# Sums of w_down's blocks formed during the first up projection and staged operand by operand: a hybrid decoder layer on one core

## The chip, the cores and the metric

The kernel runs on one core of one Trainium2 chip, as one program of some 31,800 instructions. The metric is device time in microseconds (us) of one execution, from the start of the program to its end; lower is better. Five engines work side by side, each in its own order: TensorE (PE in the rows, its weight loads PEld), VectorE (DVE), ScalarE (ACT), GpSimd (POOL) and SyncE (SP), which here issues all the transfers of the layer's second part. Their instructions meet through semaphores only.

## What is computed

One layer of a hybrid decoder for 2048 prompt tokens and 32 sample tokens: a combined projection feeds an S5 mixer and a gated linear attention, both go through w_o, and a ConvFFN follows. The change touches the ConvFFN alone (D = 1024, d_ff = 2816 = 22 blocks of 128):

```python
h2 = rms_norm(x, ffn_norm)
a, b = jnp.split(h2 @ w_up, 2, axis=-1)
ext = jnp.concatenate([conv0.astype(a.dtype), a], axis=1)
a_conv = conv_b
for w in range(CONV_W):
    a_conv = a_conv + conv_w[w] * ext[:, w:w + T]
x = x + (jax.nn.silu(a_conv) * b) @ w_down
```

Everything is float32. Each product is made of three passes of TensorE over operands that were split into a rounded part (hi) and a rest (lo): hi*hi, hi*lo, lo*hi.

## The kernel before, in words

**The stages.** The mixers and w_o take the first 1250 us or so. Then comes the up projection of the first half of the tokens (`up_first`, called for fb = 0 to 21, one block of 128 channels of a and of b each; three pieces of 352 columns, 48 matmuls each). Its results, the gated activations, go to DRAM as gT. The second half of the tokens goes through the up projection as 22 items ("up", j), and the down projection follows as 4 x 8 items ("down", c, j): c is a chunk of w_down's rows, j a block of 256 tokens. The chunks hold 2 * KH[c] blocks of 128 rows, KH = (2, 3, 3, 3), from row block K0[c] on.

**Seven products.** An item is a 2 x 2 block product by a scheme of Strassen's kind with seven products, made in the order 1, 2, 3, 6, 4, 7, 5; products 3 and 4 in this order belong to the item before (`last`). A product of chunk 0 is 6 matmuls of 512 columns, one of chunks 1 to 3 is 9, one of an up item 12. Each product p takes a stationary operand, prepared for each item one item ahead by `Item.step` and `prepare`, and a moving operand `R[p]`, which stays the same for all items of a chunk. After a product the next one is emitted, and only then `follow(p)`, which reads the PSUM bank: for products 1, 6 and 5 ScalarE copies it into a half tile (`S.get("H")`, t_H or pair_L in the rows; the bank is all) and VectorE adds that to the residual (r1, r2: t_L tiles loaded from x2d by `res_load(j + 1)` after product 7); the other products are added from the bank directly. The finished rows go back to x2d.

**The moving operands.** For a chunk of w_down with the four blocks b11, b12, b21, b22 (upper and lower rows, left and right 512 columns), products 1, 2, 3 use b11, b21, b22 as they are, product 7 uses b12 - b22 (`difference`), and 6, 4, 5 use sums built on it in place (`sums`). `operand(p, to)` forms the sum on VectorE, copies the block to hi on ScalarE and subtracts to lo on VectorE (`split2`), in two parts, 1024 elements a partition for the first two row blocks and 512 for the third. The raw blocks lie in six tiles `raw` (four for chunk 0), loaded all together by `down_blocks`. For chunks 1 to 3 a background generator, `gen_raw_down`, loads them from item j = 2 on and forms the differences. In the last item of a chunk (`end`) each operand is replaced right after the product that used it for the last time: this is called the exchange here. At the end of the up items the raw blocks are loaded after product 2, the differences formed after product 7, and all operands wait in the list `late` for product 7 or 5.

**What sets the order.** One program order is written by the Python loop; `Background.tick` puts steps of the generators between the products by priority and by an estimate of each engine's time. SP issues its transfers strictly in that order; one whose tile is not free yet holds up all that are behind it. Tiles come from `Slots`: 43 whole tiles L of 1024 floats a partition and 6 half tiles H. `get("H")` takes a small tile or a half of a split L tile (pair_L); `open()` counts what is free. All engine operations go through one helper, so all rows have its line, L290. "M" asks for a whole tile.

## Time and profile before

| | before |
|---|---|
| median of 3 timed runs | 2475.72 us (2470.17 to 2477.51) |
| the profiled execution | 2471.15 us |
| its span in the trace | 2469.4 us |
| busy: TensorE matmuls / weight loads | 93% / 79% |
| busy: VectorE / ScalarE / GpSimd | 62% / 36% / 22% |
| mean granted clock of TensorE | 0.96 of full speed |
| DMA, mean | 133 GB/s |

The span is cut into stretches in the table of windows below: its columns are the stretch and its length in us, busy us (and instructions) of PE, PEld, DVE, ACT and POOL, the granted TensorE clock (1.00 is 2.4 GHz), the mean busy share of the 16 DMA engines, and GB/s. In a timeline a row is a run of instructions of one kind without a gap: start, us, engine, line, operation, out<-in, shape and count, and in brackets the idle time ahead of it with what ended it. An all is a PSUM bank, t_L and pair_L are tiles of the pool L, t_H one of H. The first-half up projection lies at about 1260 to 1470, the up items at 1480 to 1940, the down projection from there to the end, its chunks beginning at about 1940, 2060, 2190 and 2330.

### The profile page before, as it was taken

To read this page: it belongs to the slowest core of one execution; us is meant where nothing else is said; L and a number is where in the kernel's file an instruction comes from. 1 tells how busy PE (TensorE), PEld (TensorE's weight loads), DVE (VectorE), ACT (ScalarE), POOL (GpSimd) and SP (SyncE) were. 2 spreads that over 40 slices of the span, in tenths; PEclk is the share of its full clock that TensorE was granted. 3 is DMA by queue.
4 is the path that set the end of the run, shared out by engine and by line. 5 is a ranking of instruction groups with operands and counts; after the bars stand their busy time and mean duration, and the time that the engine had idled before them with its cause. 6 is when DMAs were issued, how large, how long until landed. Compare 5 with 4: busy or idle time off the path is not lost.

```text
span 2469.4 us, 31818 instructions
## 1 busy us (share of the span) xinstructions
PE 2305.9 (93%) x11809; PEld 1950.0 (79%) x11809; DVE 1538.3 (62%) x2727; ACT 898.6 (36%) x1634; POOL 538.5 (22%) x645
## 2 busy tenths in 40 slices
PE   7898999899999799999989998999999787989898
PEld 5677777677877699999989996887888565767677
DVE  7777457765533476654454336666666777676777
ACT  3242244444422633342151114444434333242444
POOL 5254325545422345521011100000000000000011
PEclk9899999989999899999989999999999898989999
DMA  6134455427453815435422212232223474646544
GB/s 167 60 101 136 135 158 160 124 87 222 133 166 121 270 49 150 113 112 167 145 99 78 68 55 68 78 93 86 77 77 102 146 255 148 231 158 222 179 159 155
DMA packets 345260, 327.99 MB, mean 133 GB/s; under 512 B 55410, under 2 KB 273706, under 8 KB 345104
## 3 DMA queue, kind: packets, MB, share of 16 engines
q1 hardware_dynamic: 344752, 325.81, 42.6%
q8 instruction: 93, 1.52, 0.3%
q14 instruction: 63, 0.52, 0.1%
q10 hardware_dynamic: 352, 0.15, 0.0%
HBM read 230.81 MB, written 95.08 MB: 132 GB/s over the span
## 4 chain that ended last, share of the span: by engine, by line
PE 59%; DVE 18%; ACT 7%; issue 4%; POOL 2%; DMA 1%; SPq 0%; POOLq 0%; ACTq 0%; DVEq 0%
PE all L290 40%; DVE t_L L290 14%; PE mm L290 12%; PE bg L290 8%; ACT t_L L290 6%; DVE t_H L290 2%; DVE pair_L L290 2%; POOL t_H L290 2%; POOL t_L L290 1%; DMA t_L<-x2d 0%; SPq L290 0%; ACT t_H L290 0%; DMA ydT<-t_L 0%; POOL pair_L L290 0%; DMA t_H<-in_x_prompt_dram 0%
## 5 line engine op out<-in xcount | busy, mean ns | idle before, releaser
L290 PE MATMUL all<-t_L,t_L 128*128 128x512 f32 (+4 forms) x7358 | 1495.2, 365 | 80.8 <-ACT t_L L290 24.8
L290 PEld LDWEIGHTS all<-t_L,t_L 128*128 128x128 f32 (+2 forms) x7358 | 1296.7, 191 | 272.3 <-DVE t_L L290 37.5
L290 DVE TENSOR_TENSOR t_L<-t_L,t_L 128x1024 fp32r<-128x1024 f32 (+7 forms) x649 | 567.0, 902 | 178.1 <-ACT t_L L290 157.0
L290 ACT ACTIVATE t_L<-t_L 128x1024 fp32r<-128x1024 f32 (+9 forms) x471 | 374.4, 817 | 480.8 <-DVE t_L L290 399.8
L290 PE MATMUL mm<-t_L,t_L 128*128 128x512 f32 (+2 forms) x2160 | 493.2, 385 | 14.3 <-DVE t_L L290 12.3
L290 PEld LDWEIGHTS mm<-t_L,t_L 128*128 128x128 f32 (+1 forms) x2160 | 383.7, 191 | 100.0 <-issue 17.7
L290 POOL TENSOR_SCALAR rr<-ss 128x1 f32<-128x1 f32 (+1 forms) x51 | 19.7, 387 | 1098.9 <-ACT t_H L290 1093.6
L290 DVE TENSOR_TENSOR t_L<-t_L,all 128x512 f32<-128x512 f32 (+2 forms) x268 | 172.3, 643 | 112.9 <-PE all L290 51.8
L290 POOL TENSOR_SCALAR t_L<-t_L 128x1024 fp32r<-128x1024 f32 (+1 forms) x91 | 116.6, 1287 | 319.8 <-PE all L290 113.8
L290 POOL TENSOR_TENSOR t_L<-t_L,t_L 128x1024 fp32r<-128x1024 f32 x49 | 136.4, 2786 | 51.0 <-ACT t_L L290 38.8
L290 ACT ACTIVATE t_L<-all 128x512 f32<-128x512 f32 (+2 forms) x134 | 71.6, 539 | 185.9 <-PE all L290 185.5
L290 DVE TENSOR_TENSOR t_L<-t_L,t_H 128x512 f32<-128x512 f32 (+4 forms) x148 | 90.2, 611 | 77.0 <-ACT t_H L290 49.8
L290 DVE SCALAR_TENSOR_TENSOR t_L<-all,cw,t_L 128x351 f32<-128x351 f32 (+1 forms) x132 | 74.9, 567 | 72.5 <-ACT t_L L290 71.7
L290 ACT ACTIVATE t_H<-all 128x512 f32<-128x512 f32 (+2 forms) x105 | 61.5, 589 | 155.7 <-PE all L290 155.4
L290 PE MATMUL bg<-t_L,t_L 128*128 128x256 f32 (+7 forms) x628 | 110.0, 341 | 2.3 <-DVE t_H L290 2.3
L290 PEld LDWEIGHTS bg<-t_L,t_L 128*128 128x128 f32 (+4 forms) x628 | 84.1, 181 | 24.4 <-issue 10.9
L290 ACT ACTIVATE t_L<-all,cw 128x352 f32<-128x352 f32 x66 | 42.4, 642 | 165.8 <-PE all L290 161.0
L290 ACT ACTIVATE t_L<-bg 128x512 fp32r<-128x512 f32 (+7 forms) x121 | 53.5, 462 | 106.3 <-PE bg L290 103.9
L290 DVE SCALAR_TENSOR_TENSOR t_L<-t_L,cw,t_L 128x1024 f32<-128x1024 f32 x44 | 56.5, 1285 | 24.6 <-ACT t_L L290 23.8
L290 ACT ACTIVATE t_H<-t_L 128x1024 bf16<-128x1024 f32 (+2 forms) x60 | 57.0, 959 | 28.1 <-DVE t_L L290 18.2
L290 ACT ACTIVATE junk<-bg 128x128 bf16<-128x128 f32 (+1 forms) x68 | 18.8, 276 | 117.1 <-PE bg L290 115.5
L290 ACT ACT_TABLE_LOAD x41 | 52.6, 1283 | 23.1 <-DVE t_L L290 14.8
(178 smaller groups left out, 1608.9 us busy)
## 6 DMA issues: line engine op xcount, KB each, us to landing
t_L<-in_w_up_dram SPq DMA_DIRECT2D x88, 512.0 KB, 4.8
t_L<-x2d SPq DMA_DIRECT2D x80, 512.0 KB, 5.7
t_L<-in_w_in_dram SPq DMA_DIRECT2D x64, 512.0 KB, 5.7
x2d<-t_L SPq DMA_DIRECT2D x48, 512.0 KB, 3.2
gT<-t_L SPq DMA_DIRECT2D x44, 512.0 KB, 2.7
t_L<-gT SPq DMA_DIRECT2D x48, 384.0 KB, 4.1
t_L<-in_w_o_dram SPq DMA_DIRECT2D x24, 512.0 KB, 5.3
t_L<-in_w_down_dram SPq DMA_DIRECT2D x22, 512.0 KB, 4.4
```

Source lines behind the costliest of these rows:

```text
L290: r = fn(*args, **kw)
```

## The change

Two things are done. First, a background generator `gen_sums` runs beside `up_first`. For each of the 11 pairs of row blocks (upper and lower half of a chunk) it loads two whole rows of blocks of w_down, forms the four blocks 12 - 22, 11 + (12 - 22), and so on with four VectorE operations of 512, and stores the two tiles to a new DRAM tensor `Wd`. Second, `raw`, `Columns`, `down_blocks` and `gen_raw_down` are gone; `operand` now serves only the up items. `down_block` loads the block of a single operand, in the order of `STAGES`, from w_down for operands 1, 2 and 3 and from `Wd` for 6, 7, 5 and 4 (one whole tile, and a half tile for the third row block). `gen_stage_down` loads three of them from item j = 2 on; `down_operand` splits a staged block into hi and lo, gives its tiles back, and `next_block` then issues the load of the next. At the end of the up items the first two loads are issued after products 1 and 2, and operands are made from product 3 on. The list in `t = [S.get("M")] + [S.get("H")] * (kh - 2)` calls `S.get("H")` once also for kh = 2, where the result is not kept.

```diff
+    Wd = drp.tile([NF // 2, 2, P, SM], F32, tag="Wd", name="Wd")
...
-    def down_blocks(q):
-
-        kh = KH[q]
-        raw.extend(S.get("L") for _ in range(6 if kh == 3 else 4))
...
-    def gen_raw_down(q):
-        while raw or S.open() < 6.0 or S.whole() < 6:
-            yield "idle"
-        down_blocks(q)
-        yield raw
-        difference(Columns(q))
+    stage, staged = {}, []
+    STAGES = (1, 2, 6, 7, 5, 3, 4)
+
+    def down_block(p, q):
+
+        kh, k0 = KH[q], sum(KH[:q])
+        n = min(kh, 2)
+        t = [S.get("M")] + [S.get("H")] * (kh - 2)
+        if p in (1, 2, 3):
+            r0, c0 = (K0[q] + (kh if p > 1 else 0)) * P, 512 * (p == 3)
+            src = w_down[r0 : r0 + kh * P, c0 : c0 + 512].rearrange("(k p) c -> p k c", p=P)
+        else:
+            src = Wd[k0 : k0 + kh, p < 6, :, 512 * (p in (5, 7)) :][:, :, :512].rearrange("k p c -> p k c")
+        SP.dma_start(t[0][:, :1024].rearrange("p (k c) -> p k c", k=2), src[:, :2])
         if kh == 3:
...
+            SP.dma_start(t[1][:, :512], src[:, 2])
+        stage[p] = t
+        staged.append(p)
+
+    def next_block(q):
+        if len(staged) < 7:
+            down_block(STAGES[len(staged)], q)
+
+    def down_operand(p, q):
+
+        room_for(p, KH[q])
+        t = stage.pop(p)
+        split2(R[p][0][:, :1024], R[p][1][:, :1024], t[0][:, :1024])
+        if KH[q] == 3:
+            split2(R[p][2][:, :512], R[p][2][:, 512:1024], t[1][:, :512])
+        S.put(*t)
+
+    def gen_stage_down(q):
+
+        for p in STAGES[:3]:
+            while S.open() < 1.5 or S.whole() < 2:
+                yield "idle"
+            down_block(p, q)
+
+    def gen_sums():
+
+        for q in range(4):
+            for k in range(KH[q]):
+                while S.open() < 3.0 or S.whole() < 2 or not all(("st", 1, i) in flags for i in "abc"):
+                    yield "idle"
+                S_ = Share(S, 2.0)
+                a, b = S_.get("M"), S_.get("M")
+                for t, r in ((a, K0[q] + k), (b, K0[q] + KH[q] + k)):
+                    SP.dma_start(t[:, :D], w_down[r * P : (r + 1) * P])
+                yield a, b
+                lo, hi = slice(0, 512), slice(512, 1024)
+                sub(a[:, hi], b[:, hi], a[:, hi])
+                add(a[:, lo], a[:, lo], a[:, hi])
+                sub(b[:, hi], b[:, hi], a[:, lo])
+                sub(b[:, lo], b[:, lo], a[:, lo])
+                yield a, b
+                for i, t in enumerate((a, b)):
+                    SP.dma_start(Wd[sum(KH[:q]) + k, i], t[:, :SM])
...
             if p in (3, 4):
-                if refill:
-                    operand(p, refill)
-            elif end and kind == "up":
-                room_for(p, to)
+                if refill is not None:
+                    down_operand(p, refill)
+                    next_block(refill)
...
+            elif end:
+                room_for(p, KH[to])
+                if kind == "up":
+                    for q in {1: 2, 2: 2}.get(p, 0) * "x":
+                        next_block(to)
                 late.append(p)
...
-            elif end:
-                operand(p, to)
+                while late and late[0] in stage and (p not in (1, 2) or kind == "down"):
+                    q = late.pop(0)
+                    down_operand(q, to)
+                    next_block(to)
...
-                nxt = [bg.add(2, gen_raw_down(c + 1))]
+                nxt = [bg.add(2, gen_stage_down(c + 1))]
```

TensorE's order stays the same, instruction by instruction. VectorE in the last item of chunk 1, around product 6, before: t_L_17140 to t_L_17145 are the raw blocks, rows of 768 and 384 are the preparation of the next item, rows with all or t_H read a bank's result into the residual.

```order
L290 TENSOR_TENSOR t_L_17432<-t_L_17432,t_L_17574 128x384 x2
L290 TENSOR_TENSOR t_L_17452<-t_L_17452,all_17468 128x512
L290 TENSOR_TENSOR t_L_17639<-t_L_17432,t_L_17638 128x768
L290 TENSOR_TENSOR t_L_17140<-t_L_17141,t_L_17140 128x1024
L290 TENSOR_TENSOR t_L_13012<-t_L_17140,t_L_13011 128x1024
L290 TENSOR_TENSOR t_L_17144<-t_L_17144 128x512
L290 TENSOR_TENSOR t_L_16680<-t_L_17144,t_L_16680 128x512
L290 TENSOR_TENSOR t_L_17563<-t_L_17563,t_H_17657 128x512
```

The same place after: t_L_17238, 17242 and 17262 are staged blocks of operands 1, 2 and 6, pair_L_17239 and pair_L_15945 their half tiles.

```order
L290 TENSOR_TENSOR t_L_11359<-t_L_17238,t_L_11358 128x1024
L290 TENSOR_TENSOR t_L_16740<-pair_L_17239,t_L_16740 128x512
L290 TENSOR_TENSOR t_L_17654<-t_L_17654,pair_L_17701 128x512
L290 TENSOR_TENSOR t_L_17705<-t_L_17667,t_L_17704 128x768
L290 TENSOR_TENSOR t_L_11403<-t_L_17242,t_L_11402 128x1024
L290 TENSOR_TENSOR t_L_16762<-pair_L_17239,t_L_16762 128x512
L290 TENSOR_TENSOR t_L_17654<-t_L_17654,all_17691 128x512
L290 TENSOR_TENSOR t_L_17525<-t_L_17525,t_L_17667 128x384 x2
L290 TENSOR_TENSOR t_L_17545<-t_L_17545,all_17561 128x512
L290 TENSOR_TENSOR t_L_17738<-t_L_17525,t_L_17737 128x768
L290 TENSOR_TENSOR t_L_13123<-t_L_17262,t_L_13122 128x1024
L290 TENSOR_TENSOR t_L_16791<-pair_L_15945,t_L_16791 128x512
L290 TENSOR_TENSOR t_L_17656<-t_L_17656,pair_L_17758 128x512
```

The two sums (t_L_17140<-t_L_17141,t_L_17140 and t_L_17144<-t_L_17144) are gone from between the subtractions; the subtractions stand where they stood.

SyncE in the same exchange, before: the loads of the residuals from x2d and of the activations from gT, and the stores of finished rows.

```order
L290 DMA t_L_17561<-x2d 128x1024
L290 DMA t_L_17563<-x2d 128x1024
L290 DMA t_L_17663<-gT 128x6x128
L290 DMA t_L_17665<-gT 128x6x128
L290 DMA x2d<-t_L_17452 128x1024
L290 DMA x2d<-t_L_17454 128x1024
L290 DMA t_L_17706<-x2d 128x1024
L290 DMA t_L_17708<-x2d 128x1024
L290 DMA t_L_17786<-gT 128x6x128
L290 DMA t_L_17788<-gT 128x6x128
```

The same stretch of SyncE after; the rows with Wd or in_w_down_dram load staged blocks.

```order
L290 DMA t_L_17688<-Wd 128x2x512
L290 DMA pair_L_17239<-Wd 128x512
L290 DMA t_L_17712<-Wd 128x2x512
L290 DMA pair_L_17239<-Wd 128x512
L290 DMA x2d<-t_L_17545 128x1024
L290 DMA t_L_17745<-in_w_down_dram 128x2x512
L290 DMA pair_L_15945<-in_w_down_dram 128x512
L290 DMA t_L_17764<-gT 128x6x128
L290 DMA t_L_17766<-gT 128x6x128
L290 DMA x2d<-t_L_17547 128x1024
L290 DMA t_L_17787<-Wd 128x2x512
L290 DMA pair_L_17239<-Wd 128x512
```

Four blocks, each of a whole tile and a half tile, are now loaded between these; three of the four half tiles are the same one, pair_L_17239, so that each load of it stands behind the subtraction that reads it.

SyncE in the first-half up projection around fb = 13, before: t_L<-in_w_up_dram are the weights of a coming fb, gT<-t_L the results of one.

```order
L290 DMA t_L_11143<-in_w_up_dram 128x8x128
L290 DMA t_L_11149<-in_w_up_dram 128x8x128
L290 DMA gT<-t_L_10833 128x1024
L290 DMA gT<-t_L_10833 128x32
L290 DMA t_L_11472<-in_w_up_dram 128x8x128
L290 DMA t_L_11478<-in_w_up_dram 128x8x128
L290 DMA gT<-t_L_11151 128x1024
L290 DMA gT<-t_L_11151 128x32
```

The same stretch of SyncE after, with the pairs of w_down's rows and of Wd's tiles in it.

```order
L290 DMA t_L_11657<-in_w_up_dram 128x8x128
L290 DMA t_L_11701<-in_w_up_dram 128x8x128
L290 DMA gT<-t_L_11497 128x1024
L290 DMA gT<-t_L_11497 128x32
L290 DMA Wd<-t_L_11653 128x1024
L290 DMA Wd<-t_L_11654 128x1024
L290 DMA t_L_11798<-in_w_down_dram 128x1024
L290 DMA t_L_11799<-in_w_down_dram 128x1024
L290 DMA t_L_11864<-in_w_up_dram 128x8x128
L290 DMA Wd<-t_L_11798 128x1024
L290 DMA Wd<-t_L_11799 128x1024
L290 DMA t_L_11910<-in_w_down_dram 128x1024
```

Loads of w_down and stores of Wd have come between; each store of Wd waits for VectorE's four operations on its tile, and what is behind it on SP waits too.

## Rows read from the trace of the kernel before

**Rows 1.** The page's first part: busy us, share of the span, instructions.
```profile
PE 2305.9 (93%) x11809; PEld 1950.0 (79%) x11809; DVE 1538.3 (62%) x2727; ACT 898.6 (36%) x1634; POOL 538.5 (22%) x645
```
**Rows 2.** Windows: stretch, us, busy PE PEld DVE ACT POOL, PEclk, DMA share, GB/s.
```profile
1260.00:1300.00 40.00, 31.06 (x173) 29.95 (x172) 26.95 (x57) 20.80 (x43) 3.67 (x6) 0.83 0.05 18
1300.00:1440.00 140.00, 140.00 (x880) 140.00 (x879) 55.19 (x144) 21.57 (x43) 13.53 (x13) 1.00 0.23 72
1860.00:1920.00 60.00, 59.50 (x260) 48.34 (x259) 39.04 (x51) 25.68 (x33) 0.00 (x0) 1.00 0.33 107
1920.00:1960.00 40.00, 26.70 (x88) 19.43 (x87) 30.66 (x44) 14.39 (x21) 0.00 (x0) 0.83 0.36 110
1980.00:2040.00 60.00, 50.71 (x211) 40.45 (x209) 44.41 (x77) 22.30 (x42) 0.00 (x0) 0.91 0.79 260
2040.00:2080.00 40.00, 28.11 (x93) 21.08 (x94) 31.91 (x48) 16.36 (x25) 0.00 (x0) 0.79 0.36 118
2100.00:2160.00 60.00, 60.00 (x266) 47.57 (x265) 40.74 (x62) 17.53 (x27) 0.00 (x0) 1.00 0.68 228
2160.00:2220.00 60.00, 50.92 (x190) 40.13 (x189) 47.77 (x69) 24.80 (x36) 0.00 (x0) 0.86 0.51 160
2300.00:2360.00 60.00, 49.60 (x195) 39.34 (x194) 48.41 (x71) 26.20 (x39) 0.73 (x2) 0.91 0.53 170
```
**Rows 3.** TensorE's timeline around the exchange for chunk 2, 2150 to 2230.
```profile
2149.66 28.72 PE L290 MATMUL all<-t_L,t_L 128*128 128x512 f32 x126
2182.54 9.06 PE L290 MATMUL all<-t_L,t_L 128*128 128x512 f32 x27 [4.16 <-ACT t_H L290]
2193.48 12.14 PE L290 MATMUL all<-t_L,t_L 128*128 128x512 f32 x45 [1.88 <-ACT t_H L290]
2207.93 0.73 PE L290 MATMUL all<-t_L,t_L 128*128 128x512 f32 x2 [2.31 <-ACT t_L L290]
2209.39 20.80 PE L290 MATMUL all<-t_L,t_L 128*128 128x512 f32 x78 [0.73 <-DVE t_L L290]
```
**Rows 4.** Windows of 5 us, in the hole at 1995 and after two stops.
```profile
1995.00:2000.00 5.00, 0.00 (x0) 0.00 (x0) 0.09 (x1) 0.00 (x0) 0.00 (x0) 0.70 1.07 395
2180.00:2185.00 5.00, 2.46 (x6) 1.98 (x7) 4.25 (x7) 3.62 (x6) 0.00 (x0) 0.63 0.01 2
2195.00:2200.00 5.00, 5.00 (x16) 3.96 (x15) 5.00 (x8) 3.03 (x4) 0.00 (x0) 0.66 0.39 97
```
**Rows 5.** VectorE's timeline, 2150 to 2230.
```profile
2168.64 1.83 DVE L290 TENSOR_TENSOR t_L<-t_L,t_L 128x1024 fp32r<-128x1024 f32 x2 [0.34 <-ACT t_L L290]
...
2179.45 1.23 DVE L290 TENSOR_TENSOR t_L<-t_L,t_L 128x1024 fp32r<-128x1024 f32 x1 [1.18 <-ACT t_L L290]
2180.60 0.69 DVE L290 TENSOR_TENSOR t_L<-t_L 128x512 f32<-128x512 f32 x1
...
2182.04 0.69 DVE L290 TENSOR_TENSOR t_L<-t_L,t_L 128x512 fp32r<-128x512 f32 x1 [0.76 <-ACT t_L L290]
```
**Rows 6.** ScalarE's timeline, 2150 to 2230.
```profile
2181.38 0.63 ACT L290 ACTIVATE t_L<-t_L 128x512 fp32r<-128x512 f32 x1 [1.95 <-DVE t_L L290]
2181.91 0.58 ACT L290 ACTIVATE t_H<-all 128x512 f32<-128x512 f32 x1
...
2212.78 0.60 ACT L290 ACTIVATE t_H<-all 128x512 f32<-128x512 f32 x1 [1.89 <-PE all L290]
```
**Rows 7.** VectorE's groups by line and form, 1480 to 2470.
```profile
L290 DVE TENSOR_TENSOR t_L<-t_L,t_L 128x512 f32<-128x512 f32 x97 | 64.8, 687 | 0.8
```
**Rows 8.** Timeline of VectorE and SP's queue around the hole at 1995.
```profile
1984.16 3.49 SPq L290 DMA_DIRECT2D t_L<-in_w_down_dram  x6
...
1992.53 0.88 SPq L290 DMA_DIRECT2D t_L<-x2d  x2
...
1999.91 0.69 DVE L290 TENSOR_TENSOR t_L<-t_L,t_H 128x512 f32<-128x512 f32 x1 [7.40 <-DMA t_L<-x2d]
```
**Rows 9.** The page's DMA issues: KB each, median us to landing.
```profile
t_L<-x2d SPq DMA_DIRECT2D x80, 512.0 KB, 5.7
...
t_L<-in_w_down_dram SPq DMA_DIRECT2D x22, 512.0 KB, 4.4
```

More of the change, by code (lines that the diff above doesn't have):

```diff
@@ L1641 @@
     class Windows:
-        slots, parts, early = 4, 2, True
+        slots, parts = 4, 2
         def block(self, b, g):
@@ L1731, in difference, with room_for @@
             sub(o.block(1, g), o.block(3, g), o.block(1, g))
-    def room_for(p, o):
+    def room_for(p, n):
         R.setdefault(p, [])
-        while len(R[p]) > o.slots:
+        while len(R[p]) > n:
             S.put(R[p].pop())
-        while len(R[p]) < o.slots:
+        while len(R[p]) < n:
             R[p].append(S.get("L", F32R))
@@ L1752, in operand @@
     def operand(p, o):
-        room_for(p, o)
+        room_for(p, o.slots)
         for g in range(o.parts):
-            if not (o.early and p in (6, 4)):
+            if p not in (6, 4):
                 sums(p, o, g)
@@ L2460, in product @@
         bg.tick()
-    def down_blocks(q):
-        kh = KH[q]
-        raw.extend(S.get("L") for _ in range(6 if kh == 3 else 4))
-        for t in raw:
-            clock.split_tile(t, SL, (0, 512, SL))
-        for b in range(4):
-            r0 = (K0[q] + b // 2 * kh) * P
-            c0 = b % 2 * 512
-            SP.dma_start(raw[b][:, :1024].rearrange("p (k c) -> p k c", k=2), w_down[r0 : r0 + 2 * P, c0 : c0 + 512].rearrange("(k p) c -> p k c", p=P))
-        if kh == 3:
-            for i in range(2):
-                r0 = (K0[q] + i * kh + 2) * P
-                SP.dma_start(raw[4 + i][:, :1024], w_down[r0 : r0 + P])
@@ new lines, in gen_sums @@
+    def gen_sums():
[16 more added lines that the diff above has]
+                    SP.dma_start(Wd[sum(KH[:q]) + k, i], t[:, :SM])
+                S_.put(a, b)
+                S_.end()
+        flags.add("sums")
@@ L2573, in conv_states @@
         S.put(*co)
-    early = [bg.add(2, gen_raw())] + [bg.add(3, gen_build(i)) for i in half_tiles(1)] + [bg.add(3, gen_early())]
+    early = [bg.add(4, gen_sums()), bg.add(2, gen_raw())] + [bg.add(3, gen_build(i)) for i in half_tiles(1)] + [bg.add(3, gen_early())]
     for fb in range(NF):
@@ L2599 @@
         first = (kind, j) == ("up", 0)
-        to = Windows() if first else Columns(0) if kind == "up" else Columns(min(c + 1, 3))
         if end and kind == "down":
             bg.drain(*nxt)
+        to = 0 if kind == "up" else c + 1
         x = Up(it) if kind == "up" else Down(it)
@@ L2607 @@
                 for q in {1: (6,), 2: (7,), 6: (5,), 7: (3, 4)}.get(p, ()):
-                    operand(q, to)
+                    operand(q, Windows())
                 if p == 7:
@@ L2622 @@
             if p in (3, 4):
-                if refill:
-                    operand(p, refill)
-            elif end and kind == "up":
-                room_for(p, to)
-                late.append(p)
-                if p == 2:
-                    down_blocks(0)
-                elif p == 7:
-                    difference(to)
-                if p in (7, 5):
-                    for q in late:
-                        operand(q, to)
-                    late.clear()
-            elif end:
-                operand(p, to)
+                if refill is not None:
+                    down_operand(p, refill)
+                    next_block(refill)
+                    if p == 4:
+                        staged.clear()
+            elif end:
[3 more added lines that the diff above has]
+                        next_block(to)
+                late.append(p)
+                while late and late[0] in stage and (p not in (1, 2) or kind == "down"):
+                    q = late.pop(0)
+                    down_operand(q, to)
+                    next_block(to)
         queue[:] = [q_ for q_ in queue if q_.ready or q_.at < 6]
         last, refill = x, to if end else None
+        assert not late
         if kind == "down" and j == 2:
```

9 lines of the change are left out of this document (removed).

## The prediction

> **What bounds the kernel now.** I read the page first: TensorE is busy for 93% of the span [rows 1], so there is something to win only where it stands still or runs slowly. The table by stretches comes next, because it shows where. In the first half's up projection (1300 to 1440) TensorE is busy in every microsecond while VectorE needs 55 of 140 [rows 2]. In the second half the steady stretches are full too: 260 matmuls in 60 us in the up projection, 266 in the down projection, clock 1.00 [rows 2]. The gaps lie where the moving operands in R are exchanged for the next chunk of w_down. At the steady rate of their own stage, the exchange at 1920 to 1960 lacks 85 of 173 matmuls, those at 2040, 2160 and 2300 lack 84 of 177, 76 of 266 and 71 of 266 [rows 2]. In time: 19.5, 19.0, 17.1 and 16.0 us, together 71.6. A fifth hole, 1980 to 2040, lacks 55 of 266, 12.4 us [rows 2].
>
> The exchange at 2160, for chunk 2, is the one to follow. TensorE stops for 4.16, 1.88, 2.31 and 0.73 us [rows 3], 9.1 of the 17.1; the other 8 are clock, which falls from its upper level of 2.4 GHz towards 1.2 after each stop (0.63 and 0.66 on average in 5 us [rows 4]). The first two stops end on a ScalarE copy t_H<-all, the reading of a PSUM bank into which the next product accumulates. That copy is a short one, at 2181.91, right behind a 512-wide conversion [rows 6]; and the conversions stand in ScalarE's queue waiting for VectorE, which first has to form the sum (1.95 us of waiting before the second conversion). VectorE in turn waits 1.18 and 0.76 us for ScalarE's conversions [rows 5]. So each of the three summed operands costs a ping-pong of two engines, with the bank's copy queued behind.
>
> **The change part by part.** *The exchange for chunks 2 and 3.* Removed are the three sums of 1024 and 512 elements (for products 6, 5 and 4; the two differences were formed ahead, in the chunk's body). They take 1.15 us from start to start (2179.45 to 2180.60) and 0.69, of which, overlapped alike, some 0.6 counts [rows 5]: 1.75 per operand, and the waits 1.18 + 0.76 go with them: 3.7 us per operand, 11.1 in all. What stays is seven conversions on ScalarE and seven subtractions of 1.75 on VectorE, 12.2 us, beside an item's own VectorE work, 40.7 us per 266 matmuls, so 9.6 per item of 63 matmuls [rows 2]. One item takes TensorE 14.2 us. I laid the after rows of VectorE's order (quoted ahead) along these durations, from the first product of the last item: the subtraction for operand 1 is done at 4.9 us, for 2 at 8.0, for 6 at 13.3, for 7 at 17.5, for 5 at 20.3. Each is needed one item later, so none is late. The copy that product 5 waits for ends at 12.7 where product 5 could begin at 12.0: a stop of about 1 us. The other late thing is the residual x2d of the next chunk's first item. Its load stands in SP's queue behind the store of the tile before and the load for operand 4, whose half tile is free only when a subtraction is done, about 17.6; it lands 5.7 us after issue [rows 9], near 23.7, where VectorE wants it at 21.5. That is 2.2 us, nearly all of which reaches TensorE: 3 us of stops. Stops of 1.9 to 4.2 us cost another 1.7 to 3.4 in clock [rows 3, 4]; I take 3.5 for both. Remaining: 6.5. Gains 17.1 - 6.5 = 10.6 and 16.0 - 6.5 = 9.5.
>
> *The exchange for chunk 1.* A chunk-0 item is only 42 matmuls, 9.5 us, and its VectorE work 7.7, so the same splits leave VectorE behind: the copy before product 5 ends at 11.2 instead of 8.0. Stop 3.3, the residual 2.2, clock 3.5: 9. Gain 10.0.
>
> *The exchange for chunk 0.* Here sums and difference (4 x 1.15) stood inside the exchange, and all operands waited until the end of product 7; now blocks 1 and 2 are issued at product 1, and the first three operands are formed at product 6. Left is the last up item's convolution on VectorE, inside short chunk-0 items. I take 6 us of stops and 3.5 of clock. Gain 10.0. At the far ends none of it goes, or all but 2 us.
>
> *The hole at 1995.* TensorE does nothing for 5 us [rows 4] since VectorE waits 7.40 us for x2d, issued at 1992.53 behind six w_down loads, 3.15 MB [rows 8, 9]. Staging issues three blocks there, 2.36 MB, 0.79 less. Between 1984.16 and 1999.91 the queue moved at least those six loads and two residuals, 4.2 MB [rows 8, 9]: 267 GB/s or more, so 0.79 MB less lands at most 2.9 us earlier. Gain 2.7; clock left as it is.
>
> *The sums in the first half.* Eleven times four 512-wide operations of 0.69 [rows 7]: up to 30 us of VectorE, placed between fb 13 and 20, where VectorE is 39% busy and TensorE is full [rows 2]; that stretch rises to some 60%. Its cover is the PSUM queue: four pairs of banks. If the cover fails, the price is that of 1260 to 1300, where VectorE at 27 of 40 us went with 9 us lost [rows 2]. Store and load add 23 MB each way in pairs, on a queue at 23%. On SP's queue a Wd store waits for VectorE, and the next w_up load waits behind it; these loads come 35 to 50 matmuls later than before but still 150 ahead of their use. I take 2, with 0 and 9 as ends.
>
> *Slots.* With KH = 2 the list `[S.get("H")] * (kh - 2)` is empty, but S.get has been called: seven half tiles are taken and never put back, all six t_H and half of a pair, 3.5 whole tiles. From chunk 0 on the copies write pair_L halves out of tiles just freed, some still being stored. No row shows that wait. Its nearest rows are t_H copies that ended on TensorE alone [rows 6] (0) and a store's landing, which a copy with two products' slack hides: I take 5, with 0 and 30 as ends. An upside (less than 0) is out: fewer tiles free nothing.
>
> The sum: 10.6 + 9.5 + 10.0 + 10.0 + 2.7 = 42.8 gained, 7 lost: 35.8. The profiled execution took 2471.15 (span 2469.4), so 2435.4. The three timed runs have their median 4.6 above it; taking half of that, **2438**.
>
> The stops are priced above from rows. On the clock the Trainium skill says, in "TensorE: Matmul & The Clock Gate", Part 1, that the throttled level is the default and activity releases it. The trace agrees that short stops are not free: 1.88 us was followed by 0.66 [rows 3, 4].
>
> **The rivals.**
> *Only busy time goes.* If ScalarE and VectorE go on waiting for each other (item steps also alternate between them), the gain is the sums alone: 3 x 5.25 for chunks 1 to 3 and 4.6 for chunk 0, 20, less 7 for slots and first half: 2460. For it: VectorE is at 80% in these stretches [rows 2]. Against: the conversions no longer depend on sums.
> *Staged loads come late.* Four blocks of 0.79 MB are loaded inside each exchange, with the residuals behind them. If the 1995 hole repeats at chunks 1 to 3 (5 us dark, then a low clock, about 10 against the 3.5 I allow), it takes 20 back: 2458. For it: that hole [rows 8]. Against: the exchanges run the queue at 36 to 53% now, and the 5 us of the hole moved 395 GB/s [rows 2, 4]. "DMA: Bandwidth & Descriptors", Measured, in the Trainium skill wants 1 MiB per transfer for three quarters of peak and gives a fixed 2 us each; by it, as an estimate, the eight loads one behind another would take some 23 us and this rival would hold. The 395 GB/s, with 0.5 MB pieces, says they overlap.
> *Almost nothing remains.* Stops under a microsecond leave the clock alone and 2 us per exchange: 71.6 - 8 + 2.7 - 2 = 64: 2409.
> *First-half sums on the path.* All 30 us there, 28 more than I allow: 2466.
> *Slower: copies wait for stores.* For want of 3.5 tiles, a copy in each of the 24 items of chunks 1 to 3 waits for a store. A stop of 1.9 with 1.7 of clock, as at 2191 [rows 3, 4], is 3.6 per item. Twelve items eat the gain; all 24 cost 86, and with the 42.8 gained and 2 in the first half: 2519.
>
> **How the numbers follow.** Chances: forecast 0.52, only busy time 0.14, late loads 0.12, almost nothing remains 0.10, first half 0.05, slower 0.07. The range 2412 to 2466 holds the forecast, the first two rivals and half of the fourth; outside lie 2519 and most of 2409, under 0.2. A measurement here tells 0.3%, 7.4 us, from no change: below 2468.3 is faster. Of the rivals that end near 2460 some spill over: faster 0.83, same 0.09, slower 0.08.
>
> **What would show it.** Right: matmuls missing at the four exchanges fall from 85, 84, 76, 71 to some 30 to 42; ScalarE's conversions there no longer end on VectorE; the hole at 1995 shrinks to under 4 us; 1300 to 1440 stays at 140 busy. Wrong: VectorE waiting for Wd or x2d at the exchanges (late loads), ScalarE's copies ending on a DMA inside chunks 1 to 3 (slots), or TensorE idle between fb 13 and 20.

## The result, and the profile after

The changed kernel takes 2435.40 us (median of 4 runs, 2422.25 to 2440.21) against 2473.56 for the kernel before in the same comparison: a ratio of 0.985, interval 0.982 to 0.987, 38 us less. The forecast was 2438, in a range of 2412 to 2466. The profiled execution, the slowest of the four, took 2440.21 us; its span is 2438.5.

The page of the changed kernel, first part; it answers to [rows 1].

```profile
PE 2291.6 (94%) x11809; PEld 1939.5 (80%) x11809; DVE 1541.9 (63%) x2743; ACT 897.5 (37%) x1634; POOL 539.9 (22%) x645
```

TensorE does the same 11809 matmuls. VectorE is busy as long as before: the sums were moved, not saved.

Windows of the changed kernel, columns as in [rows 2]. The exchanges lie up to 30 us earlier than before, so the stretches are moved with them.

```profile
1300.00:1440.00 140.00, 140.00 (x867) 140.00 (x868) 89.23 (x179) 23.07 (x45) 14.35 (x13) 0.99 0.65 220
1920.00:1960.00 40.00, 29.97 (x121) 22.88 (x120) 30.07 (x43) 19.83 (x27) 0.00 (x0) 0.96 0.52 167
1980.00:2030.00 50.00, 44.60 (x194) 36.39 (x192) 35.06 (x64) 18.80 (x36) 0.00 (x0) 0.93 0.81 262
2030.00:2080.00 50.00, 42.15 (x170) 32.12 (x169) 42.28 (x65) 23.96 (x38) 0.00 (x0) 0.97 0.74 249
2080.00:2140.00 60.00, 60.00 (x266) 47.55 (x265) 40.04 (x61) 17.35 (x27) 0.00 (x0) 1.00 0.69 219
2155.00:2215.00 60.00, 55.50 (x236) 44.62 (x235) 50.02 (x75) 28.36 (x43) 0.00 (x0) 0.97 0.71 227
2285.00:2345.00 60.00, 55.28 (x234) 44.37 (x233) 52.27 (x77) 30.42 (x49) 3.00 (x6) 0.97 0.69 217
```

The exchanges for chunks 2 and 3 lack 30 and 32 matmuls of 266 where it was 76 and 71 [rows 2]: 6.8 and 7.2 us. Chunk 0's lacks 52 of 173 (85 before), and from 2030 to 2080, around chunk 1's, 52 of 222 are missing, 11.7 us. The clock in them is 0.96 to 0.97 (0.79 to 0.91 before). The steady stretch at 2080 still has 266 in 60 us. In the first half VectorE needs 89 of 140 us instead of 55, with TensorE as full as before, but slower at first, right after a stop that ends at 1299.82 (867 matmuls instead of 880).

TensorE runs the same matmuls in the same order in every kernel here. So the start of the n-th matmul can be compared between two traces, which puts each gain in its place. Taken from the traces, in us against the kernel before (less is earlier): the difference at matmul 6600, counted from the zero of each trace (some 11 us ahead of the span's start), and then its growth in each stretch.

```
                 at 6600   first-half   up items   exchange    hole at   exchange   exchange   exchange   9700 to
                           sums         7000-9700  chunk 0     1995      chunk 1    chunk 2    chunk 3    the end
after               5.9       2.3          0.4       -7.4       -1.4      -10.8      -10.5       -8.8      -38.9
sums_back           1.0       1.6         -0.8       -1.2       -1.7       -4.4       -6.3       -3.2      -16.8
sums_ahead          5.1       1.6         -0.8       -2.6       -3.9       -7.2       -7.2       -5.8      -26.8
sums_parts          3.7       1.8         -0.6       -1.3       -2.4       -0.2        0.4       -0.7       -4.3
before_reorder      4.6       0.4         -2.9        0.9       -0.8       -4.3       -5.6       -4.3      -14.1
mend                1.5       2.4          0.5       -8.4       -0.7      -11.0      -12.5      -10.8      -43.4
res_first           2.7       3.3         -0.2       -8.0       -2.2      -10.7      -13.4      -12.2      -46.5
mend_res            4.5       1.2         -0.2       -7.9       -2.0      -10.8      -12.5      -11.2      -44.4
combo              -4.3       1.2         -0.2       -8.0       -8.7       -7.2      -12.5      -11.3      -47.7
combo_spread        0.1       1.7         -0.5       -8.3       -8.7      -14.4      -12.5      -11.2      -55.2
combo_late          3.3       0.4          0.1       -8.0       -9.5      -14.4      -12.5      -11.2      -55.6
sums_only           2.6       1.3         -0.6        0.8       -0.8        1.2       -1.2       -0.1       -0.1
```

The bounds are matmuls 6600, 7000, 9700, 9990, 10100, 10300, 10850 and 11450. Three things stand out. In the changed kernel next to nothing is won or lost in the up items, and none (not in the table) between the exchanges, where the difference stays the same to 0.02 us from 10300 to 10650: the gain lies where the prediction put it. Before matmul 6600, ahead of all that the edits touch, single executions differ by 10 us. That is why the sums below start at 6600 or 9700, and why medians a few us apart say less than the table. And the entries, each from one execution, scatter too. sums_only has the exchanges of the kernel before and still differs from it by up to 1.2 us in one of them (the last column by 0.1). At the hole, seven kernels with the same staging (after, sums_back, sums_ahead, sums_parts, mend, res_first, mend_res) gain from 0.7 to 3.9 us.

The exchange for chunk 2 on TensorE, in the changed kernel; it answers to [rows 3].

```profile
2154.61 14.69 PE L290 MATMUL all<-t_L,t_L 128*128 128x512 f32 x64
2169.89 3.94 PE L290 MATMUL all<-t_L,t_L 128*128 128x512 f32 x16 [0.59 <-DVE t_L L290]
2175.06 2.89 PE L290 MATMUL all<-t_L,t_L 128*128 128x512 f32 x11 [1.22 <-ACT pair_L L290]
2180.63 19.58 PE L290 MATMUL all<-t_L,t_L 128*128 128x512 f32 x79 [2.68 <-DVE t_L L290]
```

Three stops of 4.5 us in all instead of four of 9.1. What the last two wait for stands in the timeline of all engines at that place.

```profile
2169.86 0.38 SPq L290 DMA_DIRECT2D t_L<-Wd  x1
...
2170.89 0.68 DVE L290 TENSOR_TENSOR t_L<-pair_L,t_L 128x512 fp32r<-128x512 f32 x1
...
2171.60 0.33 SPq L290 DMA_DIRECT2D pair_L<-Wd  x1
2171.99 1.39 SPq L290 DMA_DIRECT2D t_L<-x2d  x2
2173.69 0.68 DVE L290 TENSOR_TENSOR t_L<-pair_L,t_L 128x512 fp32r<-128x512 f32 x1
2174.41 0.60 ACT L290 ACTIVATE pair_L<-all 128x512 f32<-128x512 f32 x1 [3.89 <-DVE t_L L290]
...
2179.01 0.69 DVE L290 TENSOR_TENSOR t_L<-t_L,pair_L 128x512 f32<-128x512 f32 x1 [2.56 <-DMA t_L<-x2d]
```

The bank's copy at 2174.41 writes a half tile that the subtraction at 2173.69 has just finished reading; that is the 1.22. The residual's load is issued at 2171.99, behind a half-tile load that SyncE could issue only at 2171.60, when the subtraction at 2170.89 was done; VectorE waits 2.56 us for it, TensorE 2.68.

### The profile page after: what moved, and what is told of

It is laid out like the page before. It is cut to its first block, busy times and chain, and to the rows that moved or that the text cites. A ratio compares the mean times of both kernels' runs of the same rounds, so it can differ in the third digit from the quotient of the medians.

```text
span 2438.5 us, 32038 instructions
## 1 busy us (share of the span) xinstructions
PE 2291.6 (94%) x11809; PEld 1939.5 (80%) x11809; DVE 1541.9 (63%) x2743; ACT 897.5 (37%) x1634; POOL 539.9 (22%) x645
## 4 chain that ended last, share of the span: by engine, by line
PE 61%; DVE 15%; ACT 6%; issue 4%; POOL 3%; DMA 2%; SPq 0%; POOLq 0%; DVEq 0%; ACTq 0%
PE all L290 41%; PE mm L290 11%; DVE t_L L290 11%; PE bg L290 8%; ACT t_L L290 5%; DVE t_H L290 2%; DVE pair_L L290 2%; POOL t_H L290 2%; DMA t_L<-x2d 1%; POOL t_L L290 1%; POOL pair_L L290 1%; ACT t_H L290 0%; DMA t_L<-gT 0%; SPq L290 0%; ACT pair_L L290 0%
## 5 line engine op out<-in xcount | busy, mean ns | idle before, releaser
L290 PE MATMUL all<-t_L,t_L 128*128 128x512 f32 (+4 forms) x7358 | 1476.6, 362 | 62.1 <-DVE t_L L290 31.1
L290 PEld LDWEIGHTS all<-t_L,t_L 128*128 128x128 f32 (+2 forms) x7358 | 1283.2, 189 | 248.5 <-DVE t_L L290 46.8
L290 DVE TENSOR_TENSOR t_L<-t_L,t_L 128x1024 fp32r<-128x1024 f32 (+9 forms) x636 | 552.4, 894 | 173.9 <-ACT t_L L290 140.1
L290 ACT ACTIVATE t_L<-t_L 128x1024 fp32r<-128x1024 f32 (+8 forms) x450 | 361.9, 826 | 452.7 <-DVE t_L L290 370.8
L290 DVE TENSOR_TENSOR t_L<-t_L,pair_L 128x512 f32<-128x512 f32 (+2 forms) x138 | 92.6, 674 | 70.8 <-ACT pair_L L290 52.0
L290 ACT ACTIVATE pair_L<-all 128x512 f32<-128x512 f32 (+1 forms) x104 | 61.6, 594 | 163.9 <-PE all L290 139.1
L290 PEld LDWEIGHTS bg<-t_L,t_L 128*128 128x128 f32 (+4 forms) x628 | 84.9, 182 | 24.6 <-issue 10.9
L290 DVE TENSOR_TENSOR gS<-gS,bg 128x128 f32<-128x128 f32 x32 | 9.1, 284 | 81.5 <-ACT junk L290 81.5
```

What stands on the lines that cost most here:

```text
L290: r = fn(*args, **kw)
```

## The experiments

Eleven kernels were run, each timed against the kernel before (whose median was 2472 to 2474 in these lots). before_reorder and sums_only start from the kernel before, the other nine from the changed kernel.

**sums_back: the sums' work put back.**

```diff
+    def same(t, q):
+
+        for x, n in zip(t, (1024, 512)):
+            x = x[:, :n]
+            tt(x, x, x, ALU.max)
...
         t = stage.pop(p)
+        if p in (6, 5, 4):
+            same(t, q)
         split2(...)
```

> The changed kernel, with three VectorE operations put back into every exchange: the staged block of products 6, 5 and 4 is replaced by the maximum of itself and itself (1024 and 512 elements wide, in place) right before its conversion to hi. The data stay what they were; work and order are those of the sums that the change took out. Theory (the sums cost their own 1.75 us and make ScalarE and VectorE wait for each other): each exchange of chunks 1 to 3 loses most of the 9 to 11 us that it had gained, chunk 0's some 4, so 25 to 35 us over the changed kernel's 2435, 2460 to 2470. Rival 1 (only busy time counts): 3 x 5.25 and 3.5, 19 us, 2454. Rival 2 (the gain is that of staging blocks one by one, the sums were hidden): within 5 us of 2435.

Measured: 2458.10 us (ratio 0.9945, 0.993 to 0.996). At the exchanges 16.8 of the 38.9 us are left, so 22.1 went (23 by the medians). That is between the theory's 25 to 35 and the 19 of busy time alone, and it rules out that the sums were hidden. It left the question what the 16.8 were.

**sums_ahead: the same work one operand earlier.**

```diff
             split2(...)
+        n = {2: 6, 7: 5, 3: 4}.get(p)
+        if n:
+            same(stage[n], q)
         S.put(*t)
```

> The same three operations as in sums_back, each one operand earlier: behind the split of products 2, 7 and 3, on the staged block that is converted next. VectorE has the same work, but no conversion waits for an operation right in front of it. Theory (waiting for each other matters beside the work): clearly less lost than in sums_back, 8 to 18 us over 2435. Rival 1 (only busy time): as much as sums_back, within 3 us. Rival 2 (staging): within 5 us of 2435.

Measured: 2449.40 us (0.991, 0.989 to 0.994), 14 above the changed kernel and 9 below sums_back; at the exchanges 26.8 are left. The same VectorE work costs 12.1 us when no conversion stands right behind it, and 22.1 when one does. Of this difference of 10.0, 2.2 lie at the hole, where the two kernels do the same and the table scatters; the other 7.9 lie at the exchanges. The theory's 8 to 18 holds; busy time alone, which forecast no difference, does not.

**mend and res_first: the two stops that are left.**

```diff
-        t = [S.get("M")] + [S.get("H")] * (kh - 2)
+        t = [S.get("M")] + [S.get("H") for _ in range(kh - 2)]
```

> The changed kernel with the half tile taken only where there is a third row block, so that the six t_H and the half of a pair are not lost. Theory, from the trace of the changed kernel: in the chunks' bodies TensorE is full already (90 matmuls in 20 us), so nothing is won there; at the exchanges one stop of 1.2 us ends on a bank copy into a half tile that a subtraction still reads, and the residual's load waits on SyncE behind the load into such a half tile. Without that 2 to 4 us per exchange of chunks 1 to 3: 5 to 12 us below 2435. Rival (want of tiles costs in every item, as the prediction allowed): 5 us or more, spread over the bodies. Rival (other things are late there anyway): within 3 us of 2435.

```diff
+            if end and p == 7 and kind == "down":
+                while FS.left < 2.0 and bg.relieve():
+                    pass
+                res_load(0)
             if kind == "down" and p == 7 and j < 7:
...
-                res_load(0)
+                if 0 not in res:
+                    res_load(0)
```

> The changed kernel with the residual rows of the next chunk's first item loaded after product 7 of the last item, as for all other items, so ahead of the last staged blocks on SyncE. Theory: the stops that end with VectorE's wait for x2d (2.56 us for TensorE's 2.68 at chunk 2, 2.91 at chunk 3, 1.3 at chunk 1) go, with the clock that follows them 2.5 to 4 us per exchange: 8 to 11 us below 2435. Rival (VectorE is late at this place by its own queue, the residual only hides it): 0 to 3 us.

Measured: mend 2432.22 (0.984, 0.981 to 0.987), res_first 2430.09 (0.984, 0.981 to 0.987). By the table mend wins 4.5 and res_first 7.6 more than the changed kernel from 9700 on, at chunks 2 and 3 above all. Both fall short of what was expected: 5 to 12 us below 2435 for mend (3.2 by the medians), 8 to 11 for res_first (5.3). At chunk 1 res_first wins nothing: its expectation put 1.3 us there on the residual, but the stop of 1.34 is still there, and in the changed kernel no engine waits for a transfer at that exchange. TensorE at the exchange for chunk 2 in res_first, then in mend:

```profile
2166.39 3.94 PE L290 MATMUL all<-t_L,t_L 128*128 128x512 f32 x16 [0.59 <-DVE t_L L290]
2171.55 2.89 PE L290 MATMUL all<-t_L,t_L 128*128 128x512 f32 x11 [1.22 <-ACT pair_L L290]
2174.70 8.47 PE L290 MATMUL all<-t_L,t_L 128*128 128x512 f32 x36 [0.26 <-DVE t_L L290]
2183.72 16.62 PE L290 MATMUL all<-t_L,t_L 128*128 128x512 f32 x72 [0.55 <-DVE t_L L290]
```

```profile
2165.83 6.41 PE L290 MATMUL all<-t_L,t_L 128*128 128x512 f32 x27 [0.59 <-DVE t_L L290]
2173.16 5.96 PE L290 MATMUL all<-t_L,t_L 128*128 128x512 f32 x25 [0.92 <-DVE t_L L290]
2179.40 2.35 PE L290 MATMUL all<-t_L,t_L 128*128 128x512 f32 x9 [0.28 <-ACT t_H L290]
2182.01 0.74 PE L290 MATMUL all<-t_L,t_L 128*128 128x512 f32 x2 [0.26 <-ACT t_L L290]
2184.09 16.16 PE L290 MATMUL all<-t_L,t_L 128*128 128x512 f32 x70 [1.34 <-DVE t_L L290]
```

In res_first the 2.68 has become 0.26 and the 1.22 stays; the stops are 2.6 us in all. In mend the 1.22 is gone and the 2.68 has become 0.92, but three smaller stops follow, 3.4 us in all. So the lost half tiles cost nothing inside the chunks, as the up items and the stretches between the exchanges show, but 4.2 us at the exchanges of chunks 1 to 3.

**sums_parts: the old order of the sums.** sums_back had both operations ahead of both conversions, the kernel before had part by part.

```diff
-    split2(R[p][0][:, :1024], R[p][1][:, :1024], t[0][:, :1024])
-    if KH[q] == 3:
-        split2(R[p][2][:, :512], R[p][2][:, 512:1024], t[1][:, :512])
+    for g, (x, n) in enumerate(zip(t, (1024, 512))):
+        x = x[:, :n]
+        if p in (6, 5, 4):
+            tt(x, x, x, ALU.max)
+        split2(...)    # of this part
```

> As sums_back, with the three operations put back in the order in which the kernel before had its sums: for the two parts of an operand in turn, operation, conversion, subtraction, so that the second part's operation stands behind the first part's subtraction on VectorE. In sums_back both operations stand ahead of both conversions, and 16.7 of the 38.9 us gained at the exchanges were still there. Theory (an operand's two parts were interleaved, two rounds from VectorE to ScalarE and back instead of one): nearly the whole gain of the exchanges of chunks 1 to 3 is lost, and the time is 2463 to 2470. Rival (what sums_back kept is the gain of loading each block on its own): as sums_back, 2458 within 3 us.

Measured: 2473.24 us, ratio 1.000 (0.998 to 1.002): as slow as the kernel before, with all the staging in it. At the exchanges 4.3 us are left, of chunks 1 to 3 only 0.5: a little more was lost than expected (2463 to 2470). The timeline of VectorE and ScalarE in sums_parts, at the first of the three operands of chunk 2's exchange:

```profile
2177.43 1.22 DVE L290 TENSOR_TENSOR t_L<-t_L 128x1024 f32<-128x1024 f32 x1
2178.74 1.06 ACT L290 ACTIVATE t_L<-t_L 128x1024 fp32r<-128x1024 f32 x1 [2.22 <-DVE t_L L290]
2179.83 1.23 DVE L290 TENSOR_TENSOR t_L<-t_L,t_L 128x1024 fp32r<-128x1024 f32 x1 [1.18 <-ACT t_L L290]
2180.97 0.68 DVE L290 TENSOR_TENSOR pair_L<-pair_L 128x512 f32<-128x512 f32 x1
2181.75 0.63 ACT L290 ACTIVATE t_L<-pair_L 128x512 fp32r<-128x512 f32 x1 [1.95 <-DVE pair_L L290]
...
2182.41 0.69 DVE L290 TENSOR_TENSOR t_L<-pair_L,t_L 128x512 fp32r<-128x512 f32 x1 [0.76 <-ACT t_L L290]
```

and in sums_back:

```profile
2171.09 1.22 DVE L290 TENSOR_TENSOR t_L<-t_L 128x1024 f32<-128x1024 f32 x1
2172.22 0.69 DVE L290 TENSOR_TENSOR pair_L<-pair_L 128x512 f32<-128x512 f32 x1
2172.40 1.06 ACT L290 ACTIVATE t_L<-t_L 128x1024 fp32r<-128x1024 f32 x1 [2.22 <-DVE t_L L290]
2173.36 0.61 ACT L290 ACTIVATE t_L<-pair_L 128x512 fp32r<-128x512 f32 x1
2173.49 1.23 DVE L290 TENSOR_TENSOR t_L<-t_L,t_L 128x1024 fp32r<-128x1024 f32 x1 [0.58 <-ACT t_L L290]
...
2174.63 0.68 DVE L290 TENSOR_TENSOR t_L<-pair_L,t_L 128x512 fp32r<-128x512 f32 x1
```

The first shows the same waits, to the hundredth, as [rows 5, 6]: 1.18 and 0.76 on VectorE, 1.95 on ScalarE. In the second VectorE waits once, 0.58, and ScalarE's second conversion follows the first at once.

**before_reorder: the kernel before with that order alone.**

```diff
         for g in range(o.parts):
             if not (o.early and p in (6, 4)):
                 sums(p, o, g)
+        for g in range(o.parts):
             split2(...)
```

> The kernel before with one change: an operand's sums of both parts are formed ahead of both splits. No DRAM sums, no staging; the first operands of the up items, where a sum is formed in place too, get the same order. Theory (two rounds became one): 8 to 15 us below the kernel before's 2472, mostly at the exchanges of chunks 1 to 3. Rival (staging was what helped): within 4 us of 2472.

Measured: 2457.34 us (0.9934, 0.991 to 0.996), 17 below the kernel before in the same lot, where 8 to 15 was expected. At the exchanges of chunks 1 to 3 it wins 14.2 and in the up items 2.9. Two swapped loops give two fifths of what the change gave.

**mend_res and combo: both mends, and a later staging.** mend_res holds the edits of mend and res_first. combo moves in addition:

```diff
+        if kind == "down" and j == 4 and c < 3:
+            nxt = [bg.add(2, gen_stage_down(c + 1))]
         if kind == "down" and j == 2:
...
-            if c < 3:
-                nxt = [bg.add(2, gen_stage_down(c + 1))]
```

> The changed kernel with both the half tiles mended and the residual loaded after product 7. From 9700 matmuls on, mend gained 43.4 and res_first 46.4 us against before, the changed kernel 38.9. If the two are of different stops (1.22 on the bank's copy, 2.7 on the residual): 50 to 52 us, 2425 to 2428. If they share them: 46 to 47, about 2430.

> As mend_res, with the early staging of the next chunk's first three blocks from item 4 on instead of item 2. Theory (the hole at 1995 is the residual's load behind 2.36 MB of staged blocks): the stop of 4.4 to 5.8 us there goes with the clock that follows, 6 to 9 us below mend_res; no stop appears later, as three items are left for the loads. Rival (the samples' outputs and gT loads fill the queue there anyway): within 3 us of mend_res.

Measured: mend_res 2430.96 (0.984, 0.981 to 0.986), 44.4 us from 9700 on, where 46 to 47 was the lower of the two forecasts. The two edits share their stops, as that forecast had it, but together they give 2.1 less than res_first alone, 0.9 of it at chunk 2 and 1.0 at chunk 3: the stops there are those of mend, not of res_first. Why the mended half tiles leave longer stops than the shared one, no run shows. combo 2425.27 (0.981, 0.978 to 0.984), 5.7 below mend_res by the medians and 3.3 by the table (6 to 9 was expected): the hole at 1995 gives 8.7 instead of 2.0, but the exchange of chunk 1 gives 7.2 instead of 10.8. TensorE there:

```profile
1983.40 19.33 PE L290 MATMUL all<-t_L,t_L 128*128 128x512 f32 x84 [0.47 <-DVE t_L L290]
2005.99 6.22 PE L290 MATMUL all<-t_L,t_L 128*128 128x512 f32 x19 [3.26 <-DVE t_L L290]
```

The stop of 5.40 us at 2000.93 in the changed kernel is now one of 3.26 at 2006: a residual waits behind the three blocks there too. The expected "no stop appears later" was wrong.

**combo_spread and combo_late.** One block each at the end of items 3, 4 and 5; and, in combo_late, the first half's sums begun later.

```diff
+        if kind == "down" and c < 3 and j in (3, 4, 5):
+            down_block(STAGES[j - 3], c + 1)
```

```diff
-                while ... not all(("st", 1, i) in flags for i in "abc"):
+                while ... not all(("b", i) in flags for i in half_tiles(1)) or "early" not in flags:
```

> As combo, but the three early blocks of the next chunk are issued one each at the end of items 3, 4 and 5. In combo a stop of 3.26 us was left at 2006, behind a residual's load that took 8.2 us behind three blocks. Theory (the three blocks in a row ahead of a residual make the stop, wherever they stand): the stop goes, with its clock 4 to 6 us below combo. Rival (chunk 0's own loads fill the queue): within 2 us.

> As combo_spread, with the first half's sums begun only when the second half's first operands are formed, so that none of them stands in front of the readings of PSUM near 1300. Theory: the 2.6 us between the 6600th and the 7000th matmul go, nothing else changes. Rival (the transfers cost it, not VectorE's operations): 0.

Measured: combo_spread 2418.30 us (0.979, 0.977 to 0.981), combo_late 2418.37 (0.978, 0.977 to 0.980). With the blocks spread, the stop is 0.35 us and the exchange of chunk 1 gives 14.4:

```profile
1987.88 22.44 PE L290 MATMUL all<-t_L,t_L 128*128 128x512 f32 x97 [0.35 <-DVE t_L L290]
```

That is 7.5 us below combo by the table (4 to 6 was expected). In combo_late the stretch of the first half's sums loses 0.4 instead of 1.7 us (2.6 was expected to go), and 0.4 is also what before_reorder shows there, which has no such sums. That is too little for the medians to show. Both beat the changed kernel by 17 us, medians of two lots compared; the table has 16.3 and 16.7.

**sums_only: the first half's sums alone.** The kernel before with `gen_sums` and `Wd`, which nothing reads.

```diff
+    early = [bg.add(4, gen_sums()), bg.add(2, gen_raw())] + ...
-    early = [bg.add(2, gen_raw())] + ...
```

> The kernel before with the first half's sums added (loads of w_down, four VectorE operations a pair, stores to Wd) and nothing that reads Wd; the down projection is as before. Theory: in the changed kernel the first set of four operations stood in front of the last readings of PSUM that TensorE waited for near 1300, a stop of 6.54 us where it had been 3.88, and nothing else was lost; so 2 to 3 us more than before between the 6600th and the 7000th matmul and 0 elsewhere, 2475. Rival (the sums are on the path as a whole): up to 30 us, 2500.

Measured: 2474.35 us, ratio 1.001 (0.999 to 1.002). By the table 1.3 us are lost in the first half, less than the 2 to 3 expected. TensorE near 1300 in the kernel before, in the changed kernel, in sums_only and in combo_late:

```profile
1291.61 33.63 PE L290 MATMUL all<-t_L,t_L 128*128 128x352 f32 x193 [3.88 <-DVE aprev L290]
```

```profile
1299.82 4.40 PE L290 MATMUL all<-t_L,t_L 128*128 128x352 f32 x17 [6.54 <-DVE aprev L290]
```

```profile
1296.31 23.91 PE L290 MATMUL all<-t_L,t_L 128*128 128x352 f32 x140 [6.37 <-DVE aprev L290]
```

```profile
1294.99 25.32 PE L290 MATMUL all<-t_L,t_L 128*128 128x352 f32 x140 [3.89 <-DVE aprev L290]
```

The stop grows with the sums ahead of it and is back at 3.89 when they start later. The first of the eleven sets stood where TensorE was already waiting for VectorE; where all eleven run later (combo_late) no loss is to be seen.

## Why the prediction was right

**The sum.** From matmul 6600 on, the profiled execution gained 36.2 us; the prediction's sum was 35.8. (Its whole span is only 30.9 shorter, as the part ahead of 6600 took longer. That part varies by 10 us, so it is in part luck that the median, 2435.40, came within 3 us of the forecast.) Its terms, beside what they measured:

```
                          predicted   measured
exchange for chunk 0         10.0        7.4
hole at 1995                  2.7        1.4
exchange for chunk 1         10.0       10.8
exchange for chunk 2         10.6       10.5
exchange for chunk 3          9.5        8.8
first-half sums              -2.0       -2.3  (and 0.4 in the up items)
slots                        -5.0        0
```

**What carried it.** The step "3.7 us per operand, 11.1 in all" is borne out by sums_parts. With the sums back in their old order the exchanges of chunks 1 to 3 lost 10.6, 10.9 and 8.1 us, and the rows of the wait came back. The runs also split the 30.1 us that these three exchanges gave, by subtraction, each part with the clock that goes with it: 0.5 for the staging (sums_parts), 13.4 for the second round between the engines (sums_back less sums_parts), 6.4 for the conversion that waits right behind a sum (sums_ahead less sums_back), and 9.8 for VectorE's bare work (changed kernel less sums_ahead, which also has that work one operand earlier). So the waits that the prediction read from [rows 5, 6] were worth 19.8, twice the bare work. That is why "only busy time goes", 2460, was too high.

**The remaining stops.** At chunk 2, "a stop of about 1 us" ahead of product 5 measured 1.22, "2.2 us" of wait for the residual 2.56, and "6.5" remaining 6.8 and, at chunk 3, 7.2. The second was there for the reason given: res_first took it away. The first was not: the prediction had the copy late in ScalarE's queue. The trace has it waiting for a half tile, and in mend, where it gets another one, that stop is gone. The 6.5 itself was put together of "3 us of stops" and 3.5 of clock. By the windows above TensorE stood still for 4.5 and 4.7 us there, and 2.3 and 2.5 went to the clock: two errors that nearly cancel, so the good fit of this term is luck in part. At chunk 1 the stops were not those forecast, 3.3 before product 5 and 2.2 for the residual. There were seven, 7.9 us in all, the longest 1.72, and none of them goes back to a transfer; that the gain came out near 10.0 does not confirm the working there.

**Two more terms were mis-sized, and they cancelled.** At chunk 0 the prediction took "6 us of stops and 3.5 of clock". The changed kernel still stops there for 1.81, 0.93, 3.68, 1.29 and 2.32 us, 10.0 in all, with 2.0 of clock; the longest ends on a bank's copy, and the last on VectorE after 3.21 us of waiting for the residual:

```profile
1947.96 3.68 PE L290 MATMUL all<-t_L,t_L 128*128 128x512 f32 x8 [3.68 <-ACT pair_L L290]
...
1959.62 19.41 PE L290 MATMUL all<-t_L,t_L 128*128 128x512 f32 x84 [2.32 <-DVE t_L L290]
```

That copy stands behind the last up item's convolution on ScalarE and VectorE, which the prediction named and took too short; no run here changed it. The slots, taken at 5 inside the chunks, cost 0 there and some 4 at the exchanges, where they were already counted as a late copy and a late residual. The prediction had the loss of tiles right and its place wrong.

**The hole.** A gain of 2.7 was forecast, and a hole of under 4 us; the gain is 1.4 and the stop 5.40, where it was 6.36. TensorE before, then the changed kernel's queue, VectorE and TensorE:

```profile
2001.26 23.95 PE L290 MATMUL all<-t_L,t_L 128*128 128x512 f32 x92 [6.36 <-DVE t_L L290]
```

```profile
1984.81 0.42 SPq L290 DMA_DIRECT2D t_L<-in_w_down_dram  x1
...
1992.11 1.14 SPq L290 DMA_DIRECT2D t_L<-x2d  x2
...
1999.58 0.69 DVE L290 TENSOR_TENSOR t_L<-t_L,pair_L 128x512 f32<-128x512 f32 x1 [6.43 <-DMA t_L<-x2d]
...
2000.93 24.44 PE L290 MATMUL all<-t_L,t_L 128*128 128x512 f32 x96 [5.40 <-DVE t_L L290]
```

One execution does not settle the size. The seven kernels with this staging have stops of 3.8 to 5.8 us and gain 2.0 on average; before_reorder and sums_only, which load as before, have 6.20 and 6.25 and gain 0.8 each. The staging is then worth between 1.2 and 2.0 us, an estimate that depends on which of the old loads it is held against. Here the step that failed is that fewer bytes land sooner in proportion: the residual was used at 1999.58, nearly when it was before [rows 8], and 1.0 us earlier against TensorE's own order. The 0.79 MB are 2.3 us at the 338 GB/s that were moved from 1984 to 2000 before; it was 319 now, which takes back some 0.9 us in 16 (estimates from the two rates). Why the rate fell, no run shows. In the window the queue is full either way:

```profile
1990.00:1995.00 5.00, 5.00 (x24) 4.14 (x23) 2.56 (x5) 1.72 (x3) 0.00 (x0) 1.00 1.05 349
1995.00:2000.00 5.00, 0.53 (x3) 0.10 (x1) 0.42 (x1) 0.00 (x0) 0.00 (x0) 0.93 1.03 409
```

What decides is whether a residual is issued behind several blocks at once, as combo and combo_spread show.

**The signs.** Of the matmuls missing at the exchanges, 30 and 32 lie where "some 30 to 42" was forecast, the 52 at chunk 0 and the 52 around chunk 1 do not. At chunk 2 ScalarE's conversions of the operands no longer end on VectorE, and 1300 to 1440 stays at 140 busy. One of the signs of being wrong came in part: VectorE waits for x2d at the exchanges for chunks 2 and 3 (2.56 and 2.79 us, none before) and longer than before at chunk 0 (3.21 against 2.41). ScalarE never waits for a transfer inside chunks 1 to 3. Two small readings were wrong without consequence: the 23 MB of the first half's sums are load and store together, 11.5 each way, and the 1.15 us "from start to start" is a subtraction's [rows 5], not a sum's (a sum-sized operation took 1.22 in sums_parts).

**The rivals.** "Almost nothing remains" (2409) is about what the mends and the spread staging together reach (2418). "Staged loads come late" happened to the residuals behind the staged blocks, as said, not to the blocks. "First-half sums on the path" cost 2.3 of 30. "Slower: copies wait for stores" did not happen: nothing is lost between the exchanges. The prediction's estimate of some 23 us for eight loads one behind another rests on the fixed 2 us a transfer in the Trainium skill ("DMA: Bandwidth & Descriptors", Anatomy of one DMA, given there for transfers issued from GpSimd). At chunk 2 the eight loads were issued over 18.6 us, from 2152.96 to 2171.60, so the trace does not test that sum. But the lateness expected from it did not come: the table of waits from 1900 to 2400 has no engine waiting for a staged block (of transfers only x2d, 17.1 us in six waits, 15.0 in four before), and 409 GB/s ran with pieces of 0.5 MB and less.

## What to carry to other kernels

Where two engines pass the parts of one operand back and forth, write all of the first engine's steps ahead of the second's: the second round cost more here than the work (13.4 against 9.8 us), and swapping two loops may be had for nothing (17 us here). Work moved into a stretch where the engine has room was nearly free here (2.3 of 30 us); what it cost, it cost where its queue already held up the critical engine, so let it start after that place. On an in-order transfer queue, issue what is wanted first ahead of bulk loads and of loads whose tile isn't free, and spread bulk loads over the items.

## What the runs showed of the hardware

The mixers' part, ahead of all that the edits touch, took between 4.3 us less and 5.9 us more than in the profiled execution of the kernel before, at matmul 6600. A comparison of whole times at a few us would have taken this for an effect of the edits; comparing the n-th matmul of two traces keeps it apart. On the rest of the path the same stretch in two kernels agrees better, but not always: the exchange for chunk 2 gained 12.5 us in mend_res and in each of the three combos, which do not differ there, while sums_only, with the exchanges of the kernel before, took 1.2 us more than it at chunk 1 and 1.2 less at chunk 2. So a single entry of the table is good to about 1 us at an exchange, and to about 2 at the hole. Of TensorE's clock, the exchange for chunk 2 in the changed kernel shows that a stop need not cost any: over those of 0.59 and 1.22 us the granted clock stayed at 1.00 (2.4 GHz), and from 2178 to 2183, around the one of 2.68, it was 0.72 on average, so part of that time was at 1.2 GHz.
